# A softmax that stays in PSUM: exponentials in place, gates applied on reading, the scale in the queries

## The chip, the cores and the metric

The kernel runs on one core of one Trainium2 chip. The metric is device time in microseconds of one execution. A profile is one execution taken by the hardware profiler; its span, from the first to the last instruction, is a little shorter than the execution's own time. The engines are PE (matrix products), DVE (vector), ACT (scalar functions), POOL, and SP, which here only issues transfers. SBUF is the working memory. PSUM is the memory into which PE writes, in eight banks of 512 fp32 numbers per partition.

## What is computed

A two-layer network on 256 tokens of width 2048. The first layer is a recurrent mixer, the second an attention layer whose keys and values come in three kinds (compressed, selected, window). Every head adds three softmaxes, each weighted by a gate of its own. Cut to the part that the change touches:

```python
def block_fn(args):
    qb, gb, start = args
    s = einsum('bgrqd,bgcd->bgrqc', qb, k_cmp) * scale
    vis = cmp_end[None, :] <= tq[:, None]
    p_cmp = softmax(where(vis, s, NEG_INF), axis=-1) * any(vis, axis=-1)[:, None]
    o_cmp = einsum('bgrqc,bgcd->bgrqd', p_cmp, v_cmp)
    ...
    s = einsum('bgrqd,bgqsld->bgrqsl', qb, ks) * scale
    p = softmax(where(ok, s, NEG_INF))
    o_sel = einsum('bgrqsl,bgqsld->bgrqd', p, vs)
    ...
    s = einsum('bgrqd,bgkd->bgrqk', qb, kw) * scale
    p = softmax(where(okw, s, NEG_INF), axis=-1)
    o_win = einsum('bgrqk,bgkd->bgrqd', p, vw)
    o = gb[..., 0:1] * o_cmp + gb[..., 1:2] * o_sel + gb[..., 2:3] * o_win
```

With 256 tokens there are 4 blocks of 64 keys and up to 16 may be selected, so the selected keys are all the causal ones, and the window of 512 holds them all too. There are 15 compressed keys, 16 heads in 4 groups of 4, and a head's width is 128.

## The kernel before

Every large product is made of fp32 operands split into a high and a low half (`whi`, `wlo` for weights; `mh`, `ml` for activations; `qh`, `ql`, `kh`, `kl`, `vh`, `vl`, `Th`, `Tl` in attention), and three products are summed. For a weight tile, ACT rounds the loaded tile to the high half (line 206) and DVE subtracts it to make the low half (line 191); in the last phases every third such subtraction is given to POOL. PE needs both halves.

The matrix products of the attention layer's inputs are a list of 21 phases (`QZ`): `phase_q` makes queries for one to four heads at a time, and `phase_z` the factor that multiplies one head's output. These run as the foreground. The attention itself (`attend`, two heads at a time, from the last pair to the first) is a background generator that a planner, `Sched`, advances by estimated costs between the foreground's steps, so that its instructions are emitted among the dense products. Which instruction then follows which on each engine is decided by the framework's scheduler, from a simulated timeline of its own and the data dependences; attention's PE instructions are issued with raised priority (`atPE` is 1000). On the chip every engine runs its instructions in the order so fixed, and waits on semaphores.

One head, in `weigh`:

- PE makes the scores in two banks. `sA` (bank 5) holds the first 128 queries against the first 128 keys twice (`vA`: selected and window keys) and, in its last 32 columns, the compressed scores of both halves (`vc`). `sB` (bank 6) holds the second 128 queries against 256 keys twice (`vB`). Each of the two names has one bank, so the next head's scores can only be written when everything that reads this head's has run.
- DVE adds the causal mask to `vA` and to half of `sB` (`vD`), the visibility to `vc` (lines 1541, 1542, 1545), takes the row maxima into `mx` (1543, 1544, 1546) and multiplies `mx` by minus the scale (1547).
- ACT takes six exponentials from the banks to SBUF tiles `P0`, `P1` and `Pc` (lines 1553, 1555, 1557), each with the scale and a bias from `mx`, and sums the rows into `sm`.
- DVE takes the reciprocal into `rc` (1560), multiplies it by `anyv` and by the three gates out of `gat` (1561 to 1565), and multiplies `P0`, `P1` and `Pc` in place by `rc` (1568 to 1570).
- For the compressed part ACT rounds `Pc` into the tile `pcs` twice (1572), and DVE puts the residue beside it (1574).

`attend` then transposes the probabilities on PE (`turned`, with ACT and DVE splitting each result into `Th` and `Tl`, lines 1593 and 1598), multiplies them by the values into bank 7, and leaves `og`, which `flush` multiplies by the factor of `phase_z` on POOL (line 1640) and splits (1642 on ACT, 1643 on POOL).

`phase_q` takes the queries out of PSUM with the row factor `RS` (line 1478) and, in its first run (n = 0), computes the gates into `gat`. `rope` rotates the first 32 of 128 columns of the queries.

Of the kernel before, what the change touches and what calls it, by code (L numbers as in the profile page):

```python
# [10 lines left out]
F32 = mybir.dt.float32  # L11
F32R = mybir.dt.float32r
AF = mybir.ActivationFunctionType
OP = mybir.AluOpType
AX = mybir.AxisListType
# [8 lines left out]
NCMP = 15  # L24
GRP = 4
HEADS = 16
HID = 256
SCALE = 128 ** -0.5
# [56 lines left out]
QTB, QB, PB, TB, OGB, RPB = 1, 8, 3, 3, 1, 1  # L85
# [132 lines left out]
def hybrid_kernel(ctx: ExitStack, tc: tile.TileContext, a: dict, out: bass.AP):  # L218
    nc = tc.nc
    V, S, G, PE = nc.vector, nc.scalar, nc.gpsimd, nc.tensor  # L220
# [21 lines left out]
    def banks(**kw):  # L242
        role.update(kw)
        for n in kw:
            turn[n] = 0
# [10 lines left out]
    def accp(name="acc"):  # L256
        n = turn.get(name, 0)
        turn[name] = n + 1
        b = role[name]
        return psum.tile([128, 512], F32, name=f"bank{b[n % len(b)]}", bufs=1)  # L260
# [104 lines left out]
    def C(name):  # L365
        o, n = COLS[name]
        return cst[:, o:o + n]
# [207 lines left out]
    def rows_block(ps, nm, ncols, down=False, last=False):  # L575
        ks = range(NK)[::-1] if down else range(NK)
        for k in ks:
            yield from rows_step(ps, nm, k, W.get(), ncols, (ks[0], ks[-1]))
            if last:
                used.add((nm, k))  # L580
# [15 lines left out]
    def two():  # L596
        return [accp() for _ in range(2)]
# [727 lines left out]
    RS = [rsh[:, tt, 1:2] for tt in range(2)]  # L1325
# [7 lines left out]
    def rope(t, g, cos, sin, pool, eng, bufs=2):  # L1333
        x1, x2 = t[:, :, :, 0:16], t[:, :, :, 16:32]
        n = t.shape[1]
        cb = cos.rearrange("p (a d) -> p a d", a=n)[:, :, None, :].to_broadcast([128, n, g, 16])
        sb = sin.rearrange("p (a d) -> p a d", a=n)[:, :, None, :].to_broadcast([128, n, g, 16])
        w = [pool.tile([128, n, g, 16], F32, name=f"rp{i}", bufs=bufs) for i in range(4)]
        eng.tensor_tensor(w[0], x1, cb, op=OP.mult)
        eng.tensor_tensor(w[1], x2, sb, op=OP.mult)  # L1340
        eng.tensor_tensor(w[2], x2, cb, op=OP.mult)
        eng.tensor_tensor(w[3], x1, sb, op=OP.mult)
        eng.tensor_tensor(x1, w[0], w[1], op=OP.subtract)
        eng.tensor_tensor(x2, w[2], w[3], op=OP.add)
# [108 lines left out]
    at = tc.alloc_tile_pool(name="attn", bufs=1)  # L1453
    banks(acc=(0, 1, 2), PT=(3, 4), sA=(5,), sB=(6,), PV=(7,))
    banks(**AB)
    gat = at.tile([128, 2, 48], F32, name="gat")
    RST = at.tile([128, T], F32, name="RST")
    pr = accp("PT")
    for tt in range(2):
        rb = at.tile([128, 128], F32, name="rb", bufs=1)  # L1460
        V.tensor_copy(rb, RS[tt].to_broadcast([128, 128]))
        PE.transpose(pr[:, tt * 128:(tt + 1) * 128], rb, ident)
    V.tensor_copy(RST, pr[:, :T])
    qd, zdone, kvd, used_q = {}, {}, {}, [0]
# [4 lines left out]
    def phase_q(n):  # L1469
        h0 = QB0[n]  # L1470
        nh = QB0[n - 1] - h0
        nh = nh if n else 3
        nc_ = 128 * nh + (0 if n else 48)
        ps = two()
        yield from rows_block(ps, "u", nc_)
        t = at.tile([128, 2, 4, 128], F32, name="qt", bufs=QTB)[:, :, :nh, :]
        for tt in range(2):
            S.activation(t[:, tt], ps[tt][:, :128 * nh].rearrange("p (g d) -> p g d", g=nh), AF.Copy, scale=RS[tt])
            if n == 0:
                gl = at.tile([128, 48], F32, name="gl", bufs=2)  # L1480
                V.scalar_tensor_tensor(gl, ps[tt][:, 128 * nh:nc_], RS[tt], gbias, op0=OP.mult, op1=OP.add)
                S.activation(gl, gl, AF.Tanh, scale=0.5)
                V.tensor_scalar(gat[:, tt, :], gl, 0.25, 0.25, op0=OP.mult, op1=OP.add)
        rope(t, nh, C("cos"), C("sin"), at, V, RPB)
        sch.require(lambda: HEADS - h0 - used_q[0] <= QB)
        for g in range(nh)[::-1]:
            pt = accp("PT")[:, :T]
            for tt in range(2):
                PE.transpose(pt[:, tt * 128:tt * 128 + 128], t[:, tt, g, :], ident)
            qh = at.tile([128, T], F32R, name="qh", bufs=QB)  # L1490
            ql = at.tile([128, T], F32R, name="ql", bufs=QB)
            S.activation(qh, pt, AF.Copy)
            V.tensor_tensor(ql, pt, qh.bitcast(F32), op=OP.subtract)
            qd[h0 + g] = (qh, ql)

    def phase_z(h):
# [3 lines left out]
        z = at.tile([128, T], F32, name="zT", bufs=ZB)  # L1500
        V.tensor_tensor(z, o, RST, op=OP.mult)
        th = at.tile([128, T], F32, name="zth", bufs=2)
# [14 lines left out]
    def weigh(h):  # L1517
        PE, V, S, G = Ranked(nc.tensor, "atPE"), Ranked(nc.vector, "atE"), Ranked(nc.scalar, "atE"), Ranked(nc.gpsimd, "atE")
        g = h // GRP
        yield lambda: h in qd  # L1520
        qh, ql = qd[h]
        kh, kl = kvd[g][:2]
        sA = accp("sA")
        sB = accp("sB")
        parts = list(enumerate(((qh, kh), (qh, kl), (ql, kh))))
        for n, (q, k) in parts:
            PE.matmul(sA[:, :272], q[:, 0:128], k[:, 0, :], start=n == 0, stop=n == 2)
        for n, (q, k) in parts:
            PE.matmul(sB, q[:, 128:256], k[:, :, 0:256], start=n == 0, stop=n == 2)
            PE.matmul(sA[:, 272:288], q[:, 128:256], k[:, 0, 256:272], start=n == 0, stop=n == 2)  # L1530
        used_q[0] += 1
        sch.t += 1000
        yield 300.0
        mx = at.tile([128, 2, 3], F32, name="mx", bufs=2)
        sm = at.tile([128, 2, 3], F32, name="sm", bufs=2)
        vA = sA[:, :256].rearrange("p (x t) -> p x t", x=2)
        vB = sB.rearrange("p (s x t) -> p x s t", s=2, x=2)
        vD = sB[:, 256:].rearrange("p (x t) -> p x t", x=2)
        cb = C("caus")[:, None, :].to_broadcast([128, 2, 128])
        vc = sA[:, 256:288].rearrange("p (x c) -> p x c", x=2)[:, :, 0:NCMP]  # L1540
        V.tensor_tensor(vA, vA, cb, op=OP.add)
        V.tensor_tensor(vc, vc, C("vis").rearrange("p (x c) -> p x c", x=2), op=OP.add)
        V.tensor_reduce(mx[:, 0, 0:2], vA, axis=AX.X, op=OP.max)
        V.tensor_reduce(mx[:, :, 2], vc, axis=AX.X, op=OP.max)
        V.tensor_tensor(vD, vD, cb, op=OP.add)
        V.tensor_reduce(mx[:, 1, 0:2], vB, axis=AX.XY, op=OP.max)
        V.tensor_scalar(mx, mx, -SCALE, None, op0=OP.mult)
        yield 500.0
        P0 = at.tile([128, 2, 128], F32, name="P0", bufs=PB)
        P1 = at.tile([128, 2, 256], F32, name="P1", bufs=PB)  # L1550
        Pc = at.tile([128, 2, 16], F32, name="Pc", bufs=PB)
        for x in range(2):
            S.activation(P0[:, x], vA[:, x], AF.Exp, scale=SCALE, bias=mx[:, 0, x:x + 1], accum_out=sm[:, 0, x:x + 1])
        for t in range(2):
            S.activation(Pc[:, t, 0:NCMP], vc[:, t], AF.Exp, scale=SCALE, bias=mx[:, t, 2:3], accum_out=sm[:, t, 2:3])
        for x in range(2):
            S.activation(P1[:, x].rearrange("p (s t) -> p s t", s=2), vB[:, x], AF.Exp, scale=SCALE,
                         bias=mx[:, 1, x:x + 1], accum_out=sm[:, 1, x:x + 1])
        rc = at.tile([128, 2, 3], F32, name="rc", bufs=2)
        V.reciprocal(rc, sm)  # L1560
        V.tensor_tensor(rc[:, :, 2], rc[:, :, 2], C("anyv"), op=OP.mult)
        gv = gat[:, :, h * 3:h * 3 + 3]
        V.tensor_tensor(rc[:, :, 0], rc[:, :, 0], gv[:, :, 1], op=OP.mult)
        V.tensor_tensor(rc[:, :, 1], rc[:, :, 1], gv[:, :, 2], op=OP.mult)
        V.tensor_tensor(rc[:, :, 2], rc[:, :, 2], gv[:, :, 0], op=OP.mult)
        yield 600.0
        wide = lambda r, n: r[:, :, None].to_broadcast([128, 2, n])
        V.tensor_tensor(P0, P0, wide(rc[:, 0, 0:2], 128), op=OP.mult)
        V.tensor_tensor(P1, P1, wide(rc[:, 1, 0:2], 256), op=OP.mult)
        V.tensor_tensor(Pc[:, :, 0:NCMP], Pc[:, :, 0:NCMP], wide(rc[:, :, 2], NCMP), op=OP.mult)  # L1570
        pcs = PCS[h % 4]
        S.activation(pcs[:, :, 0:64].rearrange("p t (d c) -> p t d c", d=2)[:, :, :, 0:NCMP],
                     Pc[:, :, None, 0:NCMP].to_broadcast([128, 2, 2, NCMP]), AF.Copy)
        V.tensor_tensor(pcs[:, :, 64:64 + NCMP], Pc[:, :, 0:NCMP], pcs[:, :, 0:NCMP].bitcast(F32), op=OP.subtract)
        yield 600.0
        return P0, P1, pcs

# [173 lines left out]
```

## Time and profile before

| | us |
|---|---|
| time, median of 3 runs | 1153.34 (1150.62 to 1154.21) |
| the profiled execution's own time | 1153.73 |
| its span | 1152.0 |
| first and last start of attention's exponentials (line 1553) | 837.5, 1033.9 |

A row of a timeline gives start and duration in us, the engine, the line, what is written from what (tiles by their names in the program; `bank` is any PSUM bank, `P` is `P0` or `P1`), shapes and, in brackets, the idle time before it and what ended that. A row of a group gives line, engine, operation and count, then busy time and the mean duration of one in ns, then the idle time of the engine before them. L234 is the line of the helper through which attention's PE instructions are recorded. PEld is PE's loading of the stationary operand. The granted clock is the share of TensorE's full clock that the chip let through.

### The profile page before, as it was taken

Reading aid. Unit: us, or ns where it says so; the run is one execution under the profiler, and the core shown is the slowest. Engines: PE = TensorE matmul, PEld = TensorE weight load, DVE = VectorE, ACT = ScalarE, POOL = GpSimd, SP = SyncE. Lnnn points to the kernel's source line nnn. Section 1 sums busy time; section 2 is a strip of 40 time slices with the busy share of each in tenths; the row PEclk is TensorE's granted clock in tenths of the full one; section 3 lists DMA queues with packets and bytes.
Section 4 is the critical chain, followed back from the end, with each engine's and each line's share of the span. In section 5 each row is a group of like instructions: output and inputs, shape, how many; then the busy total and the mean of one; then the engine's idle time right before and its main releaser. Section 6 shows DMA issues by size and latency. Waiting matters only on the chain.

```text
span 1152.0 us, 25570 instructions
## 1 busy us (share of the span) xinstructions
PE 1114.9 (97%) x9398; PEld 981.0 (85%) x9398; DVE 847.5 (74%) x1836; ACT 718.4 (62%) x1697; POOL 332.1 (29%) x425
## 2 busy tenths in 40 slices
PE   7999999999999999998999999999999999999997
PEld 6878899898988888897788888887989999899887
DVE  6999976689897886566567876755567878687564
ACT  4767777677764466554547766665567666665553
POOL 1300045424347655653000010101324234333012
PEclk8999999999999999998999999999999999999999
DMA  6558878877879878774467668675745353645752
GB/s 232 155 190 242 239 205 249 241 224 218 258 219 283 210 213 243 207 190 130 131 213 254 199 194 260 201 245 160 199 136 151 97 137 90 171 102 195 280 196 97
DMA packets 232413, 226.31 MB, mean 196 GB/s; under 512 B 50608, under 2 KB 180000, under 8 KB 231904
## 3 DMA queue, kind: packets, MB, share of 16 engines
q1 hardware_dynamic: 227392, 219.73, 64.1%
q0 software_dynamic: 4896, 4.95, 1.8%
q8 instruction: 74, 1.21, 0.5%
q14 instruction: 51, 0.42, 0.1%
HBM read 200.48 MB, written 24.15 MB: 195 GB/s over the span
## 4 chain that ended last, share of the span: by engine, by line
PE 78%; DVE 11%; ACT 3%; issue 3%; DMA 2%; POOL 1%; SPq 0%; ACTq 0%; POOLq 0%; DVEq 0%
PE bank L570 13%; PE bank L569 13%; PE bank L572 13%; PE bank L587 8%; PE bank L589 7%; PE bank L588 7%; PE bank L234 3%; DVE wlo L191 3%; PE pair L572 2%; PE pair L569 1%; PE pair L570 1%; ACT whi L206 1%; PE pair L1053 1%; DVE mtmp L426 1%; PE bank L727 1%
## 5 line engine op out<-in xcount | busy, mean ns | idle before, releaser
L191 DVE TENSOR_TENSOR wlo<-wraw,whi 128x512 fp32r<-128x512 f32 (+2 forms) x616 | 438.4, 725 | 149.3 <-ACT whi L206 147.3
L206 ACT ACTIVATE whi<-wraw 128x512 fp32r<-128x512 f32 (+2 forms) x664 | 402.0, 620 | 188.8 <-PE bank L572 91.7
L587 PE MATMUL bank<-mh,whi 128*128 128x256 f32 (+1 forms) x800 | 235.2, 294 | 0.4 <-ACT whi L206 0.4
L570 PE MATMUL bank<-wlo,mh 128*128 128x512 f32 (+3 forms) x608 | 230.6, 381 | 4.5 <-DVE wlo L191 4.5
L572 PE MATMUL bank<-whi,ml 128*128 128x512 f32 (+3 forms) x608 | 228.7, 379 | 0.0
L588 PE MATMUL bank<-ml,whi 128*128 128x256 f32 (+1 forms) x800 | 227.5, 284 | 0.0
L589 PE MATMUL bank<-mh,wlo 128*128 128x256 f32 (+1 forms) x800 | 227.3, 285 | 0.0
L569 PE MATMUL bank<-whi,mh 128*128 128x512 f32 (+3 forms) x608 | 203.1, 381 | 1.6 <-ACT mh L419 0.9
L587 PEld LDWEIGHTS bank<-mh,whi 128*128 128x128 f32 (+1 forms) x800 | 151.5, 189 | 6.4 <-issue 0.9
L588 PEld LDWEIGHTS bank<-ml,whi 128*128 128x128 f32 (+1 forms) x800 | 151.8, 190 | 1.6
L589 PEld LDWEIGHTS bank<-mh,wlo 128*128 128x128 f32 (+1 forms) x800 | 151.4, 189 | 1.4
L570 PEld LDWEIGHTS bank<-wlo,mh 128*128 128x128 f32 x608 | 115.2, 190 | 23.1 <-DVE wlo L191 6.0
L569 PEld LDWEIGHTS bank<-whi,mh 128*128 128x128 f32 x608 | 114.3, 190 | 19.3 <-ACT mh L419 1.1
L572 PEld LDWEIGHTS bank<-whi,ml 128*128 128x128 f32 x608 | 115.3, 190 | 17.3
L191 POOL TENSOR_TENSOR wlo<-wraw,whi 128x512 fp32r<-128x512 f32 (+2 forms) x48 | 62.4, 1301 | 188.3 <-ACT whi L206 152.0
L570 PE MATMUL bank<-wlo,kvh 128*128 128x512 f32 x192 | 76.9, 401 | 0.0
L572 PE MATMUL bank<-whi,kvl 128*128 128x512 f32 x192 | 76.1, 396 | 0.0
L569 PE MATMUL bank<-whi,kvh 128*128 128x512 f32 x192 | 67.4, 396 | 0.0
L419 ACT ACTIVATE mh<-mtmp 128x256 fp32r<-128x256 f32 x96 | 39.2, 411 | 21.8 <-DVE mtmp L426 20.4
L426 DVE SCALAR_TENSOR_TENSOR mtmp<-xx,prm,xn 128x256 f32<-128x256 f32 x96 | 48.1, 508 | 1.2 <-POOL xx L458 1.0
L420 DVE TENSOR_TENSOR ml<-mtmp,mh 128x256 fp32r<-128x256 f32 x96 | 41.8, 444 | 2.4 <-ACT mh L419 2.2
L570 PEld LDWEIGHTS bank<-wlo,kvh 128*128 128x128 f32 x192 | 36.1, 188 | 8.7 <-issue 0.4
(332 smaller groups left out, 1871.5 us busy)
## 6 DMA issues: line engine op xcount, KB each, us to landing
wraw<-in_a_w_rkvz_dram SPq DMA_DIRECT2D x128, 512.0 KB, 5.6
wraw<-in_kv_w_dram SPq DMA_DIRECT2D x48, 512.0 KB, 4.6
wraw<-in_b_w_in_dram SPq DMA_DIRECT2D x40, 512.0 KB, 4.3
wraw<-in_a_w_o_dram SPq DMA_DIRECT2D x32, 512.0 KB, 4.6
wraw<-in_b_w_o_dram SPq DMA_DIRECT2D x32, 512.0 KB, 3.8
spd<-sp SPq DMA_DIRECT2D x16, 642.0 KB, 5.2
spl<-spd SPq DMA_DIRECT2D x16, 642.0 KB, 6.5
wraw<-in_b_w_in_dram SPq DMA_DIRECT2D x24, 384.0 KB, 3.3
```

Of the source, the lines that this page charges most:

```text
L191: eng.tensor_tensor(lv, src, hv.bitcast(F32), op=OP.subtract)
L206: self.nc.scalar.activation(hv, src, AF.Copy)
L234: return fn(*args, **kw)
L419: S.activation(h, src, AF.Copy)
L420: V.tensor_tensor(l, src, h.bitcast(F32), op=OP.subtract)
L426: V.scalar_tensor_tensor(m, xx[:, k, :], mu[:, k:k + 1], xn[:, k, 1:], op0=OP.mult, op1=OP.add)
L569: PE.matmul(o, mh[:, ts], wh[:, 0, :], start=k == ends[0], stop=False)
L570: PE.matmul(o, mh[:, ts], wl[:, 0, :], start=False, stop=False)
L572: PE.matmul(o, ml[:, ts], wh[:, 0, :], start=False, stop=k == ends[1])
L587: PE.matmul(o, wh[:, s, :], mh, start=k == 0 and first, stop=False, **kw)
L588: PE.matmul(o, wh[:, s, :], ml, start=False, stop=False, **kw)
L589: PE.matmul(o, wl[:, s, :], mh, start=False, stop=k == NK - 1, **kw)
```

## The change

Four edits, all in attention. The scale goes into the factor with which queries leave PSUM (`rsq`), so scores come out scaled. The maxima are negated by the reduction that takes them, so the multiplication of `mx` goes. The exponentials write over the scores in their banks, and the tiles `P0` and `P1` are written by the multiplication with `rc`, which reads the banks; the compressed part stays in the bank altogether and `Pc` is gone. The gates are laid out per head once, in the order of `rc` and with `anyv` multiplied in (`gate`), so that one multiplication per head takes the place of four. The compressed part is now multiplied first.

```diff
+    gate = at.tile([128, 2, HEADS, 3], F32, name="gate")
+    rsq = at.tile([128, 2], F32, name="rsq")
+    V.tensor_scalar(rsq, rsh[:, :, 1], SCALE, None, op0=OP.mult)
...
-            S.activation(t[:, tt], ps[tt][:, :128 * nh].rearrange("p (g d) -> p g d", g=nh), AF.Copy, scale=RS[tt])
+            S.activation(t[:, tt], ps[tt][:, :128 * nh].rearrange("p (g d) -> p g d", g=nh), AF.Copy, scale=rsq[:, tt:tt + 1])
...
                 V.tensor_scalar(gat[:, tt, :], gl, 0.25, 0.25, op0=OP.mult, op1=OP.add)
+                by3 = gat[:, tt, :].rearrange("p (h b) -> p h b", b=3)
+                V.tensor_copy(gate[:, tt, :, 0:2], by3[:, :, 1:3])
+                V.tensor_scalar(gate[:, tt, :, 2:3], by3[:, :, 0:1], C("anyv")[:, tt:tt + 1], None, op0=OP.mult)
...
-        V.tensor_reduce(mx[:, 0, 0:2], vA, axis=AX.X, op=OP.max)
-        V.tensor_reduce(mx[:, :, 2], vc, axis=AX.X, op=OP.max)
+        V.tensor_reduce(mx[:, 0, 0:2], vA, axis=AX.X, op=OP.max, negate=True)
+        V.tensor_reduce(mx[:, :, 2], vc, axis=AX.X, op=OP.max, negate=True)
         V.tensor_tensor(vD, vD, cb, op=OP.add)
-        V.tensor_reduce(mx[:, 1, 0:2], vB, axis=AX.XY, op=OP.max)
-        V.tensor_scalar(mx, mx, -SCALE, None, op0=OP.mult)
+        V.tensor_reduce(mx[:, 1, 0:2], vB, axis=AX.XY, op=OP.max, negate=True)
...
-        Pc = at.tile([128, 2, 16], F32, name="Pc", bufs=PB)
         for x in range(2):
-            S.activation(P0[:, x], vA[:, x], AF.Exp, scale=SCALE, bias=mx[:, 0, x:x + 1], accum_out=sm[:, 0, x:x + 1])
+            S.activation(vA[:, x], vA[:, x], AF.Exp, bias=mx[:, 0, x:x + 1], accum_out=sm[:, 0, x:x + 1])
         for t in range(2):
-            S.activation(Pc[:, t, 0:NCMP], vc[:, t], AF.Exp, scale=SCALE, bias=mx[:, t, 2:3], accum_out=sm[:, t, 2:3])
+            S.activation(vc[:, t], vc[:, t], AF.Exp, bias=mx[:, t, 2:3], accum_out=sm[:, t, 2:3])
         for x in range(2):
-            S.activation(P1[:, x].rearrange("p (s t) -> p s t", s=2), vB[:, x], AF.Exp, scale=SCALE,
+            S.activation(vB[:, x], vB[:, x], AF.Exp,
                          bias=mx[:, 1, x:x + 1], accum_out=sm[:, 1, x:x + 1])
...
-        V.tensor_tensor(rc[:, :, 2], rc[:, :, 2], C("anyv"), op=OP.mult)
-        gv = gat[:, :, h * 3:h * 3 + 3]
-        V.tensor_tensor(rc[:, :, 0], rc[:, :, 0], gv[:, :, 1], op=OP.mult)
-        V.tensor_tensor(rc[:, :, 1], rc[:, :, 1], gv[:, :, 2], op=OP.mult)
-        V.tensor_tensor(rc[:, :, 2], rc[:, :, 2], gv[:, :, 0], op=OP.mult)
+        V.tensor_tensor(rc, rc, gate[:, :, h, :], op=OP.mult)
...
-        V.tensor_tensor(P0, P0, wide(rc[:, 0, 0:2], 128), op=OP.mult)
-        V.tensor_tensor(P1, P1, wide(rc[:, 1, 0:2], 256), op=OP.mult)
-        V.tensor_tensor(Pc[:, :, 0:NCMP], Pc[:, :, 0:NCMP], wide(rc[:, :, 2], NCMP), op=OP.mult)
+        V.tensor_tensor(vc, vc, wide(rc[:, :, 2], NCMP), op=OP.mult)
+        V.tensor_tensor(P0, vA, wide(rc[:, 0, 0:2], 128), op=OP.mult)
+        V.tensor_tensor(P1.rearrange("p x (s t) -> p x s t", s=2), vB,
+                        rc[:, 1, 0:2, None, None].to_broadcast([128, 2, 2, 128]), op=OP.mult)
         pcs = PCS[h % 4]
         S.activation(pcs[:, :, 0:64].rearrange("p t (d c) -> p t d c", d=2)[:, :, :, 0:NCMP],
-                     Pc[:, :, None, 0:NCMP].to_broadcast([128, 2, 2, NCMP]), AF.Copy)
-        V.tensor_tensor(pcs[:, :, 64:64 + NCMP], Pc[:, :, 0:NCMP], pcs[:, :, 0:NCMP].bitcast(F32), op=OP.subtract)
+                     vc[:, :, None, :].to_broadcast([128, 2, 2, NCMP]), AF.Copy)
+        V.tensor_tensor(pcs[:, :, 64:64 + NCMP], vc, pcs[:, :, 0:NCMP].bitcast(F32), op=OP.subtract)
```

## The prediction

> **What bounds the kernel now.** I read the head of the page first (busy time, share of the span, instructions), then the table of stretches for attention with all engines (length, then PE, PEld, DVE, ACT, POOL busy, granted clock, DMA), then the same for TensorE alone around its gaps, then TensorE's waits there (total us, times, longest), then the timeline at the two longest (start, duration, in brackets the idle time before it and its releaser).
>
> ```profile
> span 1152.0 us, 25570 instructions
> PE 1114.9 (97%) x9398; PEld 981.0 (85%) x9398; DVE 847.5 (74%) x1836; ACT 718.4 (62%) x1697; POOL 332.1 (29%) x425
> ```
> ```profile
> 820.00:1045.00 225.00, 219.94 (x1496) 208.62 (x1495) 175.21 (x446) 146.05 (x432) 77.35 (x68) 0.98 0.49 132
> ```
> ```profile
> 917.00:920.00 3.00, 3.00 (x11) 0.50 0.85 260
> 943.00:944.00 1.00, 0.21 (x2) 1.00 0.12 42
> 985.00:988.00 3.00, 3.00 (x11) 0.50 0.85 215
> ```
> ```profile
> PE bank L570 <- DVE wlo L191: 3.1, 2, 1.7
> PE bank L1489 <- DVE qt L1344: 0.8, 1, 0.8
> PE bank L569 <- ACT whi L206: 0.7, 1, 0.7
> PE bank L234 <- DVE Tl L1598: 0.4, 1, 0.4
> ```
> ```profile
> 916.30 0.45 PE L570 MATMUL bank<-wlo,mh 128*128 128x384 f32 x1 [1.67 <-DVE wlo L191]
> ...
> 984.46 0.44 PE L570 MATMUL bank<-wlo,mh 128*128 128x384 f32 x1 [1.48 <-DVE wlo L191]
> ```
>
> PE is busy 97% of the span. The change lives between 820 and 1045 us, where PE is idle 225 - 219.94 = 5.1 us: 1.67 before 916.30, 0.7 (a weight's high half, `whi`, from ACT) and 1.48 just before 984.46, 0.8 near 943, 0.4 for a transposed weight. After the two long gaps the granted clock is 0.50 for three whole us each (917 to 920, 985 to 988), so each costs about 3 x 0.5 + 0.1 (the edges) = 1.6 us more; after the 0.8 us gap it stays at 1.00. So attention costs PE 5.1 + 2 x 1.6 = 8.3 us beyond its work. **That is all this change can win**: the amount of PE work does not change.
>
> Stall one is 1.67 + 1.6 = 3.3 us, stall two 0.7 + 1.48 + 1.6 = 3.8 us. Both end on L191, the low half of a weight tile, made by DVE. What stood ahead of it in DVE's queue, and what did POOL do meanwhile? These are the timelines of both engines at stall one, and one row of each at stall two; the last two rows, of the view of one tile, give shortest, median and longest duration in ns.
>
> ```profile
> 911.62 1.24 DVE L1568 TENSOR_TENSOR P<-P,rc 128x256 f32<-128x256 f32 x1
> 912.78 1.23 DVE L1569 TENSOR_TENSOR P<-P,rc 128x512 f32<-128x512 f32 x1
> 913.93 0.95 DVE L1514 TENSOR_TENSOR vl<-Vt,vh 128x256 fp32r<-128x256 f32 x1
> 914.80 0.97 DVE L1570 TENSOR_TENSOR Pc<-Pc,rc 128x30 f32<-128x30 f32 x1
> 915.70 0.55 DVE L191 TENSOR_TENSOR wlo<-wraw,whi 128x384 fp32r<-128x384 f32 x1
> ```
> ```profile
> 911.53 1.05 POOL L191 TENSOR_TENSOR wlo<-wraw,whi 128x384 fp32r<-128x384 f32 x1 [1.06 <-issue]
> 912.53 2.06 POOL L1643 TENSOR_TENSOR ml<-og,mh 128x256 fp32r<-128x256 f32 x2
> 914.56 1.17 POOL L191 TENSOR_TENSOR wlo<-wraw,whi 128x384 fp32r<-128x384 f32 x1
> ```
> ```profile
> 982.96 0.98 DVE L1570 TENSOR_TENSOR Pc<-Pc,rc 128x30 f32<-128x30 f32 x1
> ```
> ```profile
> 982.80 1.09 POOL L191 TENSOR_TENSOR wlo<-wraw,whi 128x384 fp32r<-128x384 f32 x1 [5.83 <-ACT whi L206]
> ```
> ```profile
> L1569 DVE TENSOR_TENSOR P<-P,rc x16: 678/687/1785, 841.2 to 1038.5; 128x512 f32<-128x512 f32 x16
> L1570 DVE TENSOR_TENSOR Pc<-Pc,rc x16: 176/484/1280, 842.9 to 1040.2; 128x30 f32<-128x30 f32 x16
> ```
>
> The softmax's gate multiplications, and they were stretched: 30 elements per row took 0.97 and 0.98 us where the fastest took 0.176, and 512 took 1.23 where the fastest took 0.678. Each of these lies beside a POOL instruction, and each reads two operands in SBUF (`P`, `rc`). An operation with one operand in PSUM is not stretched beside POOL:
>
> ```profile
> 974.96 0.68 DVE L1598 TENSOR_TENSOR Tl<-bank,Th 128x512 fp32r<-128x512 f32 x1
> ```
> ```profile
> 974.48 1.15 POOL L1643 TENSOR_TENSOR ml<-og,mh 128x256 fp32r<-128x256 f32 x1
> ```
>
> **The change, part by part.** The groups by shape over the attention window (count, then busy us and mean ns of one, then idle time before):
>
> ```profile
> L1569 DVE TENSOR_TENSOR P<-P,rc 128x512 f32<-128x512 f32 x16 | 17.0, 1060 | 0.0
> L1570 DVE TENSOR_TENSOR Pc<-Pc,rc 128x30 f32<-128x30 f32 x16 | 10.0, 625 | 0.0
> L1568 DVE TENSOR_TENSOR P<-P,rc 128x256 f32<-128x256 f32 x16 | 8.3, 519 | 0.0
> L1501 DVE TENSOR_TENSOR zT<-bank,RST 128x256 f32<-128x256 f32 x14 | 5.8, 415 | 5.2 <-PE bank L589 5.2
> L1574 DVE TENSOR_TENSOR pcs<-Pc,pcs 128x30 fp32r<-128x30 f32 x16 | 6.2, 389 | 0.0
> L1561 DVE TENSOR_TENSOR rc<-rc,cst 128x2 f32<-128x2 f32 x16 | 4.4, 276 | 0.5
> L1547 DVE TENSOR_SCALAR mx<-mx 128x6 f32<-128x6 f32 x16 | 4.3, 271 | 0.1
> ```
>
> *Multiplications out of PSUM.* P0, P1, the compressed part and the residue L1574 now have one operand in a bank. I price them by the PSUM rows of the same size: 0.415 (L1501), 0.68 (L1598 above), and 0.18 for the two of 30 elements (the fastest L1570). Before: 0.519 + 1.060 + 0.625 + 0.389 = 2.59 us a head; after: 0.415 + 0.68 + 2 x 0.18 = 1.46; less by 1.14 us, 18 us of DVE over 16 heads. Not all of it is won: an L191 standing next in the queue, with both operands in SBUF, meets the same POOL instruction. Between nothing and 18 us I count about half.
>
> [...]
>
> *Removed.* The scaling of the maximum (L1547) and three of the five little operations on `rc` (L1561 and two of L1563 to L1565). Started one behind the other they cost some 0.08 us each, about 0.3 us a head, more where POOL hits them (0.276 and 0.271 us are their means). The scale goes into `rsq` (one DVE instruction), the gates are regrouped by two copies and two multiplications, once for all heads: five small instructions in the first query block, under 5 x 0.28 = 1.4 us of DVE, not repeated.
>
> *Exponentials in place.* Six per head on ACT, now written to PSUM. No row shows ACT writing a bank. Nearest are these, which differ in the side read:
>
> ```profile
> L1642 ACT ACTIVATE mh<-og 128x256 fp32r<-128x256 f32 x13 | 5.6, 429 | 4.9 <-POOL og L1640 4.8
> L1492 ACT ACTIVATE qh<-bank 128x256 fp32r<-128x256 f32 x16 | 5.5, 386 | 2.7 <-PE bank L1489 2.7
> ```
>
> The bank is 43 ns cheaper to read, so I bound the write by 43 ns either way: 96 x 0.043 = 4 us of ACT's total, 0.26 us a head. Value taken: nothing.
>
> *What moves: the banks are held longer.* Banks 5 and 6 (`sA`, `sB`) were free for the next head's scores once ACT's last exponential had read them. Now they are free after P1 and after the residue L1574, both on DVE. One place shows what that costs:
>
> ```profile
> 936.87 0.29 PE L234 MATMUL bank<-kh,qh 128*128 128x272 f32 x1
> ```
> ```profile
> 937.01 0.42 DVE L1568 TENSOR_TENSOR P<-P,rc 128x256 f32<-128x256 f32 x1
> ...
> 939.20 0.42 DVE L1541 TENSOR_TENSOR bank<-bank,cst 128x256 f32<-128x256 f32 x1
> ```
>
> The next head's scores began at 936.87 while the previous head was still being multiplied; DVE took them up only at 939.20. After the change they begin about 0.1 + 0.34 + 0.6 + 0.2 = 1.2 us behind the start of L1568, at 938.2, and the first are usable some 1 us later, at 939.2. So the head's period hardly grows, because DVE already set it. But the scores stand in PE's queue, and dense matmuls queue behind them: if PE reaches them before DVE has freed the bank, PE idles.
>
> *Sum.* Stall one: DVE needed 915.70 - 911.62 = 4.1 us from L1568 to the late L191. Now: 0.1 + 0.34 + 0.6 + at most 0.95 (L1514) = 2.0. L191 starts 2.1 us earlier against a gap of 1.67: the stall goes, with its clock, 3.3 us. Stall two: L1570 falls from 0.98 to 0.1, and three little operations (0.24) go: 1.1 us of the 2.2. What is left is about 1.1 us of idling, near the 0.8 us that left the clock at 1.00; I take it to stay: 1.1 + 1.6 = 2.7 us. Against these, 1 us for PE waiting on a bank (now it loses 0.4 on DVE's products). 3.3 + 2.7 - 1.0 = 5.0 us. The profiled execution took 1153.73 us (span 1152.0 and 1.73 around it), 0.4 above the median: 1153.73 - 5.0 = 1148.7, on the median 1148.3; I say 1148.5.
>
> [...]
>
> **The rivals.**
> *A. Forecast*, 1146 to 1150.5: 45%.
> *B. The relief is hidden*, 1150.5 to 1156: 25%. DVE idles 225 - 175 = 50 us in this stage, so 8 to 18 us less work may mean only more idling; POOL may hit L191 in place of P1; and a new order of instructions can put other gaps of 1 to 2 us where these two were. Also here: the clock falls after what is left of stall two (1148.3 + 1.6 = 1149.9), and PE waits a little more on a bank.
> *C. The bank wait takes over*, 1156 to 1160: 20%. PE reaches the next head's scores before L1574 or P1 has released the bank. One such wait as long as stall one costs 1.67 + 1.6 = 3.3 us with its clock. From three of them in 16 heads (9.9 against 6.0 won) it is slower than before, at 1157.6; four give 1160.9. For it: the release moves from ACT, which POOL does not stretch, to the end of DVE's queue. Against it: PE already depends on DVE for every transpose of P, and loses 0.4 us on that in the whole stage.
> *D. More is won*, 1143 to 1146: 10%. All 8.3 us go, and the head's shorter chain closes the gap at 943 too.
>
> **How the numbers follow.** What measurement can tell from no change is about 0.3%, 3.5 us: faster is below 1149.9, slower above 1156.8. Faster: nearly all of A (0.41) and D (0.10): 0.51. Slower: most of C, 0.18. The rest, 0.31, lies between. The range, 1144 to 1158, leaves out the lower half of D and the upper half of C, 0.15 in all; the ends of the unknown costs (DVE relief from nothing to 18 us, exponentials 0.26 us a head either way) lie inside it, through B, C and D.
>
> **What would show it.** Right: P0, P1 and the compressed multiplication at 0.42, 0.68 and 0.18 us with almost no spread; no row of 0.50 clock between 880 and 1000; L191 no longer the releaser of a PE wait above 1 us. Wrong: PE waits at L234 on L1574's or P1's successor (case C), exponentials more than 43 ns off 0.49 us, or gaps of the same total elsewhere (case B).

## The result and the profile after

The changed kernel takes 1145.12 us (median of 8, 1143.21 to 1148.12), the kernel before 1152.10 beside it (median of 8). The ratio is 0.9939, 95% interval 0.9922 to 0.9956: faster by 0.6%, 7.0 us. A second measurement of the same kernel, beside other runs of the kernel before, gave 0.9922 (0.9908 to 0.9937), 9.1 us. The forecast of 1148.5 had the direction right; the gain was 7.0 us where about 5 were forecast.

Where did it come from? The head of the page of the changed kernel, and its table of stretches for attention (length, PE, PEld, DVE, ACT, POOL busy, granted clock, DMA):

```profile
span 1146.2 us, 25499 instructions
PE 1111.7 (97%) x9398; PEld 979.3 (85%) x9398; DVE 827.8 (72%) x1777; ACT 722.5 (63%) x1697; POOL 324.1 (28%) x425
```
```profile
820.00:1045.00 225.00, 225.00 (x1566) 215.12 (x1565) 163.09 (x396) 156.42 (x441) 73.37 (x71) 1.00 0.54 144
```

PE is busy for all 225 us and its clock never falls. Both stalls, the gap near 943 and the small ones are gone. The whole length of the last part can be read from the first product of the first query block to the last product of all (timelines of PE, before and then after):

```profile
803.99 0.44 PE L569 MATMUL bank<-whi,mh 128*128 128x432 f32 x1
...
1143.34 0.28 PE L1718 MATMUL bank<-whi,ml 128*128 128x256 f32 x1
```
```profile
808.07 0.46 PE L569 MATMUL bank<-whi,mh 128*128 128x432 f32 x1 [0.31 <-ACT Vt L1400]
...
1137.62 0.28 PE L1719 MATMUL bank<-whi,ml 128*128 128x256 f32 x1
```

It was 339.3 us and is 329.5, from start to start. Of the 9.8 us, 5.1 are PE's idle time and 3.4 its slow clock; the other 1.3 us are products that follow each other more closely, for a reason that no run shows. Up to the first of these products both programs issue the same instructions but for one small one (`rsq`), and there the changed one was 4.1 us later (808.07 against 803.99). That is the spread of single executions: another execution of the changed kernel (`e13_after_again`) was there at 802.16, and then needed the same 329.5 us. So the profiled pair differs by 5.8 us of span, and the medians by 7.0 and 9.1.

The multiplications out of the banks, and the exponentials into them (groups by shape, changed kernel):

```profile
L1570 DVE TENSOR_TENSOR P<-bank,rc 128x512 f32<-128x512 f32 x16 | 10.9, 680 | 0.0
L1569 DVE TENSOR_TENSOR P<-bank,rc 128x256 f32<-128x256 f32 x16 | 6.6, 415 | 0.0
L1568 DVE TENSOR_TENSOR bank<-bank,rc 128x30 f32<-128x30 f32 x16 | 3.1, 195 | 0.4
```
```profile
L1561 ACT ACTIVATE bank<-bank,mx 128x256 f32<-128x256 f32 x32 | 14.2, 444 | 5.1 <-DVE mx L1552 4.9
L1557 ACT ACTIVATE bank<-bank,mx 128x128 f32<-128x128 f32 x32 | 10.7, 334 | 0.4
```

680 and 415 ns are what was forecast, 195 is a little above the 180 of the sum, and nothing stretches them. The exponentials became 28 and 48 ns shorter (before: 362 and 492). So far everything looks as the prediction had it. The experiments say otherwise.

### The profile page after: what moved, and what is told of

Its sections match the earlier page's. It is cut to its first block, busy times and chain, and to the rows that moved or that the text cites. A ratio compares the mean times of both kernels' runs of the same rounds, so it can differ in the third digit from the quotient of the medians.

```text
span 1146.2 us, 25499 instructions
## 1 busy us (share of the span) xinstructions
PE 1111.7 (97%) x9398; PEld 979.3 (85%) x9398; DVE 827.8 (72%) x1777; ACT 722.5 (63%) x1697; POOL 324.1 (28%) x425
## 4 chain that ended last, share of the span: by engine, by line
PE 80%; DVE 8%; DMA 4%; issue 3%; ACT 2%; POOL 2%; SPq 0%; ACTq 0%; POOLq 0%; DVEq 0%
PE bank L570 14%; PE bank L569 13%; PE bank L572 13%; PE bank L587 7%; PE bank L588 6%; PE bank L589 6%; PE bank L234 5%; DVE wlo L191 2%; PE pair L572 2%; PE pair L569 1%; PE pair L570 1%; DVE invX L805 1%; ACT whi L206 1%; DMA spd<-sp 1%; DVE mtmp L426 1%
## 5 line engine op out<-in xcount | busy, mean ns | idle before, releaser
L191 DVE TENSOR_TENSOR wlo<-wraw,whi 128x512 fp32r<-128x512 f32 (+2 forms) x616 | 438.5, 724 | 165.6 <-ACT whi L206 159.8
L191 POOL TENSOR_TENSOR wlo<-wraw,whi 128x512 fp32r<-128x512 f32 (+2 forms) x48 | 57.5, 1197 | 187.1 <-ACT whi L206 164.0
```

What stands on the lines that cost most here:

```text
L191: eng.tensor_tensor(lv, src, hv.bitcast(F32), op=OP.subtract)
```

## The experiments

Three theories were tried in turn. Theory 1 is the prediction's: taking the multiplications out of POOL's way is what wins, and holding the banks costs little. Its rival: the small edits alone suffice. In all tables and sentences below, PE's loss is its idle time plus what the granted clock of 0.50 cost (half of the slow time), from the start of the first query product to the last product of all. A head's period is the median of the 15 steps from one head's first score product into `sA` to the next one's. A gate multiplication is called stretched when it takes over 1.2 times the shortest of its shape in its run; there are 48, three for each of 16 heads. All of these are worked out from the traces. Before: loss 5.1 + 3.4 us, period 10.3 us, 18 stretched. Changed kernel: no loss, 11.9 us, none stretched.

**All but the place** (run `e1_sbuf`): the changed kernel with exponentials in SBUF tiles and multiplied there in place.

```diff
-            S.activation(vA[:, x], vA[:, x], AF.Exp, bias=mx[:, 0, x:x + 1], accum_out=sm[:, 0, x:x + 1])
+            S.activation(P0[:, x], vA[:, x], AF.Exp, bias=mx[:, 0, x:x + 1], accum_out=sm[:, 0, x:x + 1])
...
-        V.tensor_tensor(P0, vA, wide(rc[:, 0, 0:2], 128), op=OP.mult)
+        V.tensor_tensor(P0, P0, wide(rc[:, 0, 0:2], 128), op=OP.mult)
```

> Everything of the change but the place: scale in the queries, negated maxima and the one gate multiplication stay, but the exponentials go to SBUF tiles and are multiplied there in place. Theory 1 (the gain is that the multiplications no longer share SBUF reads with POOL): stretched multiplications remain (L1569 like means near 1.0 us), at least one PE wait on L191 with a stretch of 0.50 clock remains in attention; gain under half of the change's, 0 to 3 us below before. Rival (fewer small DVE instructions and a shorter head suffice): all gaps gone, 6 to 7 us below before.

1142.59 us, ratio 0.9912 (0.9893 to 0.9931). The whole gain is there without the place. Its stretch of attention, and the view of its tile `rc` (shortest, median, longest in ns):

```profile
820.00:1045.00 225.00, 225.00 (x1572) 214.94 (x1571) 172.16 (x395) 154.00 (x443) 77.60 (x72) 1.00 0.51 140
```
```profile
L1568 DVE TENSOR_TENSOR Pc<-Pc,rc x16: 183/190/1272, 840.0 to 1022.6; 128x30 f32<-128x30 f32 x16
L1569 DVE TENSOR_TENSOR P<-P,rc x16: 410/420/1245, 840.1 to 1022.7; 128x256 f32<-128x256 f32 x16
L1570 DVE TENSOR_TENSOR P<-P,rc x16: 679/685/1232, 840.4 to 1023.0; 128x512 f32<-128x512 f32 x16
```

PE idles 0.3 us in all. Stretched multiplications are still there, up to 1.27 us for 30 elements, but they are 5 of 48 where before had 18: without the place, too, most of the stretching is gone. Theory 1 falls as a statement that the place was needed; whether the stretching mattered, this run can't say.

**The place alone** (`e2_psum`): before, with exponentials in the banks and gates applied on reading; scale, negation and the four gate operations as before.

```diff
-            S.activation(P0[:, x], vA[:, x], AF.Exp, scale=SCALE, bias=mx[:, 0, x:x + 1], accum_out=sm[:, 0, x:x + 1])
+            S.activation(vA[:, x], vA[:, x], AF.Exp, scale=SCALE, bias=mx[:, 0, x:x + 1], accum_out=sm[:, 0, x:x + 1])
...
-        V.tensor_tensor(P0, P0, wide(rc[:, 0, 0:2], 128), op=OP.mult)
+        V.tensor_tensor(P0, vA, wide(rc[:, 0, 0:2], 128), op=OP.mult)
```

> The place alone: exponentials in place in the banks and gates applied on reading, with the scale, the negation and the four small gate operations as before. Theory 1: most of the gain, 5 to 7 us below before, PE idle after the first query product under 1 us, multiplications 0.42, 0.68 and 0.19 us with no spread. Rival (small instructions): within 2 us of before, gaps remain.

1168.83 us, ratio 1.0143 (1.0123 to 1.0163): 16.8 us slower than before. Neither theory had this. The stretches and PE's waits (us, times, longest):

```profile
820.00:1050.00 230.00, 230.00 (x1571) 218.51 (x1570) 167.67 (x428) 150.68 (x415) 72.09 (x66) 1.00 0.54 150
1050.00:1100.00 50.00, 32.79 (x142) 24.93 (x141) 23.32 (x56) 20.60 (x56) 8.11 (x10) 0.86 0.31 116
```
```profile
PE bank L234 <- DVE P L1568: 5.8, 1, 5.8
PE bank L569 <- DVE h L1676: 5.7, 1, 5.7
PE bank L569 <- ACT mh L1642: 4.3, 2, 2.3
```

The two stalls of before are gone here too: no idle time at all up to 1050. But a head's period is 14.6 us where it was 10.3, so attention is still running when the dense products are used up, and then PE idles: for the last heads' probabilities (5.8), for their finished outputs (`mh`, 4.3), and for the residual `h` (5.7).

**Two one-element reads** (`e3_hold`), meant to hold the banks to the end of a head.

```diff
+        held = at.tile([128, 2], F32, name="held", bufs=2)
+        V.tensor_copy(held[:, 0:1], sA[:, 0:1])
+        V.tensor_copy(held[:, 1:2], sB[:, 0:1])
```

> Before, with the two score banks held until the head's last residue by two one-element DVE reads (0.2 us of DVE a head, about 3 us in all, added). It prices the longer hold without its relief. Theory 1 as predicted (DVE sets the head's period, the hold costs little): 0 to 3 us slower than before, PE waits at attention's matmuls under 1 us more. Rival (the hold is expensive and the change pays it out of a larger gain): 5 us slower or more, with PE waiting at the scores.

1148.12 us, ratio 0.9969 (0.9950 to 0.9987). A miss of the experiment, not of a theory: the reads depend on nothing late, and the scheduler put them right behind the exponentials, for which they wait, so the period is 10.5 us and nothing was held. What the run does show is one more order of the same work: PE still idles 4.8 us, 2.4 of it in one gap, and its clock stays at 1.00.

```profile
L1576 DVE COPY held<-bank 128x1 f32<-128x1 f32 x16 | 2.5, 156 | 9.1 <-ACT Pc L1555 9.0
```

**Another order, the same work** (`e4_shuf_before`): one planner cost of attention.

```diff
-        yield 500.0
+        yield 700.0
         P0 = at.tile([128, 2, 128], F32, name="P0", bufs=PB)
```

> Before with one planner cost of attention changed from 500 to 700, which reorders instructions and changes no work. It shows how much of 7 us an accident of order can make. Theory 1: the stretched multiplications stay and some 3 to 8 us of PE idle and slow clock stay in attention, though at other places; within 3 us of before. Rival (the two stalls were an accident of order that any reordering removes): 6 to 8 us faster, no gap over 1 us.

1150.33 us, ratio 0.9992 (0.9975 to 1.0008). The stalls survive a reordering, with 5.3 us of idle time; PE's waits and its stretches (length, PE busy, clock, DMA):

```profile
PE bank L570 <- DVE wlo L191: 3.2, 2, 1.7
PE bank L1489 <- DVE qt L1344: 1.6, 1, 1.6
```
```profile
820.00:1045.00 225.00, 219.71 (x1519) 1.00 0.49 136
917.00:920.00 3.00, 3.00 (x20) 1.00 0.99 315
```

A gap of 1.7 us is here too, behind the same L191, and the clock is 1.00 over the whole stretch. So the slow clock is not part of the stall's price in every execution; the section on the prediction has what the traces show of it.

**Theory 2**, after these: the place costs because the next head's scores must wait for the banks, and the small edits pay for it; either the negation (2a, since the multiplication of `mx` joined all maxima before any exponential) or the gates (2b).

**The hold alone** (`e6_hold2`): the two reads now depend on the residue and on P1.

```diff
+        held = at.tile([128, 2], F32, name="held", bufs=2)
+        V.tensor_tensor(held[:, 0:1], sA[:, 0:1], pcs[:, 0, 64:65].bitcast(F32), op=OP.add)
+        V.tensor_tensor(held[:, 1:2], sB[:, 0:1], P1[:, 0, 0:1], op=OP.add)
```

> Before, with the two score banks really held to the end: one DVE addition reads a score together with the residue of L1574, another a score together with P1 after its multiplication. Theory 2 (the place costs because the next head's scores must wait for the bank, the small edits pay): the period from scores to scores grows from about 10.3 us to 13 us or more, attention ends 20 us or more later, and the kernel is 6 to 18 us slower than before. Rival (the place costs by ACT and DVE working on the banks, not by the hold): period under 11.5 us, within 3 us of before.

1155.49 us, ratio 1.0033 (1.0017 to 1.0049), period 13.5 us. The period is as theory 2 had it. Attention takes 15 us longer, not the 20 or more expected, and the cost, 0.3%, is below the range, because the two early stalls are gone as well:

```profile
820.00:1045.00 225.00, 225.00 (x1560) 214.07 (x1558) 182.00 (x471) 148.71 (x428) 81.64 (x70) 1.00 0.52 143
```
```profile
PE bank L569 <- DVE h L1679: 5.6, 1, 5.6
PE bank L569 <- ACT mh L1645: 2.0, 1, 2.0
```

The loss moves from attention's middle to its end. Why the early stalls go is not shown: DVE is busier in this stretch than before (182.00 against 175.21 us), and 13 of 48 multiplications are stretched, 12.9 us in sum beyond the shortest where before had 15.0.

**The negation and the scale alone** (`e7_neg`).

```diff
-        V.tensor_reduce(mx[:, 0, 0:2], vA, axis=AX.X, op=OP.max)
+        V.tensor_reduce(mx[:, 0, 0:2], vA, axis=AX.X, op=OP.max, negate=True)
...
-        V.tensor_scalar(mx, mx, -SCALE, None, op0=OP.mult)
```

> Before with the maxima negated by their reductions and the scale in the queries, and nothing else. Theory 2a (the multiplication of mx was a join: no exponential could start until all maxima were there): scores to last exponential falls from 8.7 to about 6 us, period to about 9.3 us, 5 to 9 us below before. Rival 2b (the four gate operations are what counts): period stays above 10 us, within 3 us of before.

1143.79 us, ratio 0.9932 (0.9912 to 0.9953), period 9.1 us, loss 0.8 us. The whole gain from one edit. ACT's wait for the maxima, before and in this run:

```profile
ACT P L1553 <- DVE mx L1547: 16.7, 13, 3.0
```
```profile
ACT P L1558 <- DVE mx L1548: 4.0, 6, 0.9
ACT P L1554 <- DVE mx L1546: 2.9, 4, 1.4
```

Before, the first exponential waited for one small multiplication, and this for all three maxima and its turn in DVE's queue: 16.7 us in attention. Now each bank's exponentials wait for that bank's maxima alone, 6.9 us in all. In 10 of 16 heads `sB` is now written before `sA`, and each bank is in use for a shorter time: from the first score product into it to the last exponential out of it the median falls from 7.5 to 6.1 us for `sA` and from 7.8 to 5.0 for `sB`. From a head's very first score to its last exponential it stays as it was, 8.7 and 8.5 us; here 6 had been expected. Only 5 multiplications are stretched.

**The gates alone** (`e8_gate`).

```diff
-        V.tensor_tensor(rc[:, :, 2], rc[:, :, 2], C("anyv"), op=OP.mult)
-        gv = gat[:, :, h * 3:h * 3 + 3]
-        V.tensor_tensor(rc[:, :, 0], rc[:, :, 0], gv[:, :, 1], op=OP.mult)
...
+        V.tensor_tensor(rc, rc, gate[:, :, h, :], op=OP.mult)
```

> Before with the one gate multiplication in place of four, and nothing else. Theory 2a: 0 to 3 us below before, scores to last exponential unchanged at about 8.5 us, gaps on L191 remain. Rival 2b: 5 us or more below before, the multiplications less stretched because the queue ahead of them is shorter.

1144.53 us, ratio 0.9943 (0.9924 to 0.9963), loss 1.0 us, period 10.0. The whole gain from this edit as well, though ACT still waits 12.8 us for `mx`, 12 of 48 multiplications are stretched, and 512 elements take up to 1.79 us:

```profile
820.00:1045.00 225.00, 224.04 (x1546) 212.80 (x1545) 176.94 (x407) 150.40 (x440) 79.70 (x71) 1.00 0.51 140
```
```profile
L1568 DVE TENSOR_TENSOR P<-P,rc x16: 683/685/1790, 844.1 to 1031.3; 128x512 f32<-128x512 f32 x16
```

So neither 2a nor 2b alone: each edit by itself is enough to lose the stalls, and so was the hold. That any new order loses them is ruled out by `e4_shuf_before` and `e3_hold`, which kept 5.3 and 4.8 us of idle time. Which property of the orders without stalls matters is not shown. Once PE's loss is gone there is little left to win, so the gains do not add.

**Place and negation without the gates** (`e9_psum_neg`).

> The exponentials in their banks together with negated maxima and the scale in the queries, without the gate edit: the whole change less the gates. Theory 2a: nearly all of the rescue, period about 12 us, within 3 us of the whole change (1142 to 1148). Rival 2b: the gates are needed, period near 14 us, 1155 to 1168.

1149.76 us, ratio 0.9989 (0.9971 to 1.0007): between the two theories. Period 12.7. There is one gap, and it is new (PE's waits, DVE's waits, then the issues on SP):

```profile
PE bank L569 <- DVE h L1677: 5.6, 1, 5.6
```
```profile
DVE h L1677 <- DMA h<-hd: 6.9, 1, 6.9
```
```profile
1061.22 0.34 SPq L1669 DMA_DIRECT2D fg<-in_final_g_dram  x1
1061.61 0.43 SPq L1671 DMA_DIRECT2D h<-hd  x1
```

The residual `h` (2 MB) is loaded into memory that attention gives back (`open_fin`), behind the gain row `fg` (1 MB). It landed 11.9 us after its issue; the first addition of `h`, and through its bank PE, waited for it. In the changed kernel the load was issued at 1059.5 and landed after 10.8 us, in time. How late may attention end? First score and last product with the values, before and here:

```profile
L234 PE MATMUL bank<-kh,qh x48: 170/286/482, 831.8 to 1028.6; 128*128 128x272 f32 x16, 128*128 128x512 f32 x16, 128*128 128x16 f32 x16
L234 PE MATMUL bank<-Th,vcs x8: 392/396/477, 865.9 to 1050.5; 128*128 128x512 f32 x8
```
```profile
L234 PE MATMUL bank<-kh,qh x48: 171/288/396, 829.3 to 1031.2; 128*128 128x272 f32 x16, 128*128 128x512 f32 x16, 128*128 128x16 f32 x16
L234 PE MATMUL bank<-Th,vcs x8: 392/400/479, 866.9 to 1056.3; 128*128 128x512 f32 x8
```

218.7 us from first to last before, with no late gap; 217.7 in the changed kernel, with none; 227.0 here, with one; 233.9 with the hold alone, with two, and 246.2 with the place alone, with several.

**Theory 3**: the place lengthens the period, negation and gates shorten it, and time is lost once attention ends too late for that load.

**Place and gates without the negation** (`e10_psum_gate`).

> The exponentials in their banks together with the one gate multiplication, without the negation: the joining multiplication of mx stays. Theory 3 (the place lengthens a head's period by holding the banks, negation and gates shorten it, and time is lost only once attention ends so late that the residual's load, which waits for attention's memory, comes late): period 12.5 to 14.5 us, attention ends later than in the run with place and negation, PE waits 5 us or more for h after it; 1152 to 1164. Rival (the first stalls decide, and any edit that removes them gives the floor): 1143 to 1148.

1160.40 us, ratio 1.0084 (1.0060 to 1.0108), period 14.2; the gaps are 3.7 us for P, 2.0 for `mh` and 4.2 for `h`, this last a little under the 5 that theory 3 set. The negation is what carries the place; the gates alone do not.

**The load of the residual** (`e12_pn_h2`): place and negation, with the first 512 columns of `h` asked for first.

```diff
+        h2 = fin.tile([128, 2, D], F32, name="h2")
+        hv = hd.rearrange("(a p) c -> p a c", p=128)
+        nc.sync.dma_start(h2[:, :, 0:512], hv[:, :, 0:512])
         nc.sync.dma_start(fg, bass.AP(tensor=a["final_g"].tensor, offset=a["final_g"].offset, ap=[[0, 128], [1, D]]))
-        h2 = fin.tile([128, 2, D], F32, name="h2")
-        nc.sync.dma_start(h2, hd.rearrange("(a p) c -> p a c", p=128))
+        nc.sync.dma_start(h2[:, :, 512:], hv[:, :, 512:])
```

> Place and negation (1149.8 as it was), with the residual's load reordered: the first 512 columns of h alone are asked for first, then the gain row, then the rest. Theory 3: the 5.6 us gap before the first addition of h falls below 2 us and its slow clock goes, 4 to 7 us below the run without this edit: 1143 to 1146. Rival (what is late after attention is something else than this load): 1148 to 1151.

1143.18 us, ratio 0.9926 (0.9909 to 0.9943), against 0.9989 without the edit. Attention ends as late as before it (1056.6), PE's wait is 0.5 us and its clock stays up (behind the wait, products of 512 columns follow each other by 0.23 us; behind the wait of 5.6 us in `e9_psum_neg` by 0.43):

```profile
PE bank L569 <- DVE h L1679: 0.5, 1, 0.5
```
```profile
1061.59 0.37 SPq L1671 DMA_DIRECT2D h<-hd  x1
1062.01 0.46 SPq L1672 DMA_DIRECT2D fg<-in_final_g_dram  x1
1062.52 0.43 SPq L1673 DMA_DIRECT2D h<-hd  x1
```

**The changed kernel and its SBUF form on one chip** (`e13_after_again`, `e14_sbuf_again`).

> The changed kernel itself, once more, beside the next run on one chip. Theory 3: 1144 to 1147, attention's end just early enough, no gap over 1 us.

> The changed kernel with its exponentials in SBUF again (negation, scale and gates kept), once more. Theory 3 (both have lost all stalls, so both stand on the floor that PE's own work sets): within 3 us of the changed kernel, 1141 to 1145. Rival (the place gains something of its own): 3 us or more slower than the changed kernel.

1142.47 us (0.9922, 0.9908 to 0.9937; a little below the range expected) and 1142.86 us (0.9925, 0.9911 to 0.9940): no difference, and neither has any loss. Both stand on the floor of PE's own work. The place gains nothing of its own, and with the other edits beside it, it costs nothing. No version measured beats the changed kernel clear of the noise.

| run | place | negation | gates | period, us | PE idle + slow clock, us | stretched, of 48 | ratio |
|---|---|---|---|---|---|---|---|
| before | | | | 10.3 | 5.1 + 3.4 | 18 | 1 |
| `e4_shuf_before` (order) | | | | 10.3 | 5.3 + 0 | 14 | 0.9992 |
| `e3_hold` (two reads) | | | | 10.5 | 4.8 + 0 | 16 | 0.9969 |
| `e6_hold2` (banks held) | | | | 13.5 | 8.2 + 3.4 | 13 | 1.0033 |
| `e7_neg` | | x | | 9.1 | 0.8 + 0 | 5 | 0.9932 |
| `e8_gate` | | | x | 10.0 | 1.0 + 0 | 12 | 0.9943 |
| `e1_sbuf` | | x | x | 9.1 | 0.3 + 0 | 5 | 0.9912 |
| `e2_psum` | x | | | 14.6 | 17.6 + 6.8 | 0 | 1.0143 |
| `e9_psum_neg` | x | x | | 12.7 | 5.6 + 1.7 | 0 | 0.9989 |
| `e10_psum_gate` | x | | x | 14.2 | 10.4 + 8.5 | 0 | 1.0084 |
| changed kernel | x | x | x | 11.9 | 0 + 0 | 0 | 0.9939 |

The loss is that of one profiled execution, the ratio that of all; `e8_gate`'s profile, for one, is of an execution that took 1149.38 us and lost its time before attention.

## Why the prediction was right, and where it was not

*The ceiling held.* "That is all this change can win" was put at 8.3 us of PE's idle time and slow clock in attention. In the profiled pair all of it went (225.00 of 225.00, clock 1.00), and 1.3 us of closer packing came on top; the medians say 7.0, and 9.1 in the second measurement. The forecast let part of stall two and the small gaps stay and took 1 us for bank waits; none of these was there. But the number rests in part on luck: the place alone costs 16.8 us, which the forecast put at 1, and the small edits, which it put at next to nothing, make up for that.

*The clock term was a chance, not a price.* 1.6 us was taken for each stall from one execution, as if a gap of 0.8 us were harmless and one of 1.67 not. In `e4_shuf_before` a gap of 1.7 us left the clock at 1.00. The traces of before and of the changed kernel show what the length of a gap leaves out. In each of them the slow stretches begin whole steps of 3.41 us apart: in before at 916.65 and 984.91, 20 steps apart, each one step long. In the steps just ahead of these PE was busy 1.74 and 1.19 us, so idle for 49% and 65%; the second holds two gaps, 0.74 and 1.48 us. Counted over both traces from 30 us to the last product, in steps that ran at full clock: the four with 58 to 65% of idle time were followed by the slow clock, one of the three between 48% and 51%, and none of those with 38% or less. By this the clock behind a gap would depend on how the gap lies to the steps, and its term would have no fixed size; that this is what spared `e4_shuf_before` is an estimate and was not shown.

*The multiplications:* 0.415, 0.68 and 0.195 us almost without spread (414 to 419, 680 to 682 and 186 to 198 ns), close to the forecast. In `e1_sbuf` the medians from SBUF are 0.42, 0.685 and 0.19. But that the lost stretching is what removes the stalls is not shown. They go just as well with 12 and 13 stretched multiplications in `e8_gate` and `e6_hold2`, while `e4_shuf_before` keeps them with 14. In `e2_psum`, where they go too, the period changed with the stretching, and the two were not separated.

*The small operations were mis-sized.* "About 0.3 us a head" counted four instructions started one behind the other. The negation alone was worth the whole gain, 0.9932, and the gates alone as much, 0.9943. The multiplication of `mx` was a join, and ACT's wait for it (16.7 us in attention against 6.9) is far more than its own 0.08 us a head. That this wait was the price is argued and not shown: in `e8_gate` it stays at 12.8 us, and the gain is the same.

*The step that failed is "the head's period hardly grows, because DVE already set it".* The hold alone takes it from 10.3 to 13.5 us, the place alone to 14.6. The estimate let the next head's scores follow 1.2 us behind the start of L1568, as if the residue came at once. It comes after a round trip: ACT's copy to `pcs` follows P0's multiplication, and L1575 follows the copy. In the changed kernel the residue ends 2.1 us behind the start of L1568 (medians over the heads), and the next head's scores begin 5.2 us behind it in `sA` and 3.4 in `sB`. The round trip accounts for a part of that; what the scores wait for beyond it is not shown.

```profile
L1573 ACT ACTIVATE pcs<-bank 128x60 fp32r<-128x60 f32 x15 | 3.2, 214 | 4.1 <-DVE P L1569 4.0
L1575 DVE TENSOR_TENSOR pcs<-bank,pcs 128x30 fp32r<-128x30 f32 x15 | 2.8, 185 | 1.8 <-ACT pcs L1573 1.6
```

*Rival C, "The bank wait takes over",* was the true danger, given a chance of 20% and looked for in the wrong place. In none of the 14 traces does PE idle ahead of a score product: the scores stand later in its order instead. The loss appears at attention's end and after it, at the last heads and at a load that needs attention's memory, and the prediction's window closed at 1045, ahead of the last product with the values at 1050.5. The place alone is 1.4% slower by it. The changed kernel escapes because its attention is no longer than before, 217.7 against 218.7 us. Its period is longer (11.9 against 10.3), but one of two long steps is gone: before had steps of 30.0 and 28.8 us between heads, and the changed kernel has one of 27.1.

## What to carry to other kernels

Count a small instruction between two engines by what it joins: one that waits for three results before the next engine may take the first can be worth far more than its duration (here 0.08 us a head, and 0.7% of the kernel's time with the negation alone). Keeping data in PSUM lengthens the time for which the bank is held (with the place alone a head's period went from 10.3 to 14.6 us); ask which product needs that bank next, how many times in a row, and what starts only after the last. Where PE has lost all its idle time, edits that each win the same stall do not add (0.9932 and 0.9943 alone, 0.9912 together), so test each alone before crediting one.

## What the runs showed of the hardware

- DVE operations on two SBUF operands were stretched beside POOL. In before 30 elements took 0.97 us at 914.80, begun 0.24 us into a POOL subtraction of 1.17 us and over 0.04 us after it, and 0.98 us at 982.96, over 0.05 us after another of 1.09 us; the fastest took 0.176. In `e1_sbuf` they took 0.19 us at the median, and once 1.27 us. With one operand in a bank the same 30 took 0.195 us, and in the changed kernel none of the 48 multiplications was stretched (longest 198, 419 and 682 ns). That the stretching cost so little on the path had not been expected.
- The exponentials that write a bank were shorter than those that write SBUF: 444 against 492 ns for 256 elements, 334 against 362 for 128 (changed kernel and before). In `e12_pn_h2` they took 445 and 335. In both runs the scale has left these instructions too; the share of each in the difference is not shown. The bound of 43 ns that was set from reads was a little short of the 48.
- PE's clock fell to half for the next 3.41 or 6.83 us, in the traces of before and of the changed kernel, after the four steps of 3.41 us in which PE idled for 58 to 65%, and after one of the three with 48 to 51%. A gap of 1.67 us was followed by the slow clock in before; with one of 1.7 us in `e4_shuf_before` the clock was 1.00 from 820 to 1045.
